# Dividing one 1 MB output store of a batched matmul into three transfers that load the DMA engines unequally

## The chip, the cores and the metric

The kernel runs on one core of one Trainium2 chip. The metric is the device time of one execution in microseconds, the median over several runs. A profile of one execution goes with it. It covers a span a little shorter than the metric, and it names the engines PE (TensorE, matrix multiply), PEld (its weight loads), DVE (VectorE), ACT (ScalarE), POOL (GpSimd) and SP (SyncE, which here only issues transfers and waits). The transfers themselves are carried out by the 16 DMA engines of the core, which all queues share.

## What is computed

```python
def setup_inputs():
    batch, m, k, n = 16, 512, 512, 512
    return {
        "a": np.random.randn(batch, m, k).astype(np.float32),
        "b": np.random.randn(batch, n, k).astype(np.float32),
    }

def reference(a: np.ndarray, b: np.ndarray) -> np.ndarray:
    return np.matmul(a, b.transpose(0, 2, 1)).astype(np.float32)
```

For each of 16 batch elements, a 512 x 512 matrix is multiplied by the transpose of another. Inputs are 32 MiB of float32, outputs 16 MiB, so 48 MiB (50.33 MB) cross between HBM and the core's memory.

## The kernel before, in words

The batch is worked through in eight pairs of two elements. Five programs run beside each other and are tied together by semaphores.

**Loads (SP, L89-L105).** `load(n)` brings in one 2 MB block: for even n the a matrices of pair n/2, for odd n its b matrices. Block n goes to slot n mod 7 of the ring `ld` (NL = 7). The first two blocks are loaded in two halves. From block 7 on a load waits until DVE has begun to cast the block that had the slot (`s_cd`). SP issues the first seven loads at once (L117), and then, in the loop at L119, waits for block n, tells DVE (`s_go`), and issues load n + 6.

**Compute.** DVE casts a block to bf16 into `ha`, `wa`, `hb`, `wb` (L167-L175). PE transposes 128 x 128 tiles against an identity into `tp` (L247). ACT copies the transposed a to `ta` (L206), and DVE the transposed b to `tb` (L187). PE multiplies into `ps` (L266). ACT copies each 128 x 512 result to `ob` (L224), the output ring of NO = 7 slots of one batch element each. Partition p of a slot holds rows 4p to 4p + 3 of the output, 8 KB that lie in one piece in HBM too. ACT raises `s_out` twice per pair: after the first copy of the second element (so the first is complete), and after the last.

**Stores (L110-L115).** `store(n)` waits until `s_out` is n + 1, then writes slot n mod 7 to batch n of the output: one transfer of 128 partitions x 8 KB, which adds 16 to the semaphore `s_st[n]` when it has landed. `landed(n)` (L107) gives the semaphore and the number to wait for. POOL issues stores 0 to 7, in the order that the string `STORES` (L33) writes out: an S is a store, an O a wait for a landed store, which gives ACT a free slot of `ob` (`s_of`). SP issues stores 8 to 15. The table `LATE` (L35) puts stores 8 and 9 behind the wait for load 11, stores 10 and 11 behind load 13, and stores 12 and 13 behind load 15, the last load. Stores 14 and 15 follow (L131, L132).

**End.** SP waits for stores 9 to 14 (L133, L134). A second, otherwise empty section waits for store 15 (L279, L280), and the program ends. Slot 5 of `ob`, which store 12 reads, is not written again afterwards, since batch 19 doesn't exist.

The order around the change is therefore SP's own program order: load 15 has landed, store 12, store 13, store 14, store 15, then the waits. A transfer that SP has issued lies in a queue on each DMA engine that it uses, behind those that SP issued earlier.

Of the kernel before, what the change touches and what calls it, by code (L numbers as in the profile page):

```python
# [10 lines left out]
def kernel(  # L11
# [7 lines left out]
    P = 128  # L19
    batch, M, K = a.shape  # L20
    _, N, _ = b.shape
    J = M // P
# [7 lines left out]
    NO = 7  # L30


    STORES = "SSSSOSOSOSSOOOOOO"  # L33

    LATE = {11: (8, 9), 13: (10, 11), 15: (12, 13)}  # L35

    def sbuf(name, shape, dtype):
        return ctx.enter_context(nc.sbuf_tensor(name, shape, dtype))

    def sem(name):  # L40
        return tc.alloc_semaphore(name)

    with tc.tile_critical(no_gpsimd_drain=True):  # L43
# [8 lines left out]
        ob = sbuf("ob", [P, NO, J, N], f32)  # L52
# [6 lines left out]
        s_st = [sem(f"s_st{i}") for i in range(batch)]  # L59
# [21 lines left out]
            out=ident[:], in_=ident[:], compare_op=mybir.AluOpType.not_equal, fill=1.0,  # L81
# [23 lines left out]
                nc.sync.dma_start(ld[:, slot], src).then_inc(s_ld[slot], 16)  # L105

        def landed(n):  # L107
            return s_st[n], 16

        def store(n):  # L110
            engine = nc.gpsimd if n < STORES.count("S") else nc.sync
            engine.wait_ge(s_out, n + 1)
            engine.dma_start(  # L113
                out[n].rearrange("(p j) n -> p j n", j=J), ob[:, n % NO]
            ).then_inc(s_st[n], 16)  # L115
# [3 lines left out]
        for n in range(2 * pairs):  # L119
            got = nc.sync.wait_ge(s_ld[n % NL], 16 * (n // NL + 1))  # L120
            if n < 2:
                got.then_inc(s_go, 1)
                nc.sync.wait_ge(s_second[n], 16).then_inc(s_go, 1)
            else:
                got.then_inc(s_go, 2)

            if n > 0 and n + NL - 1 < 2 * pairs:
                load(n + NL - 1)
            for m in LATE.get(n, ()):
                store(m)  # L130
        store(batch - 2)  # L131
        store(batch - 1)  # L132
        for n in range(batch - NO, batch - 1):  # L133
            nc.sync.wait_ge(*landed(n))  # L134
# [3 lines left out]
        nc.gpsimd.wait_ge(s_ld[0], 32)  # L138
        for what in STORES:
            if what == "S":  # L140
                store(n_st)
                n_st += 1
            else:
                nc.gpsimd.wait_ge(*landed(n_of)).then_inc(s_of, 1)
                n_of += 1
# [12 lines left out]
        with nc.Fori(0, pairs, engines=[dve]) as u:  # L158
            for x, (h, w, s_c, s_w) in enumerate(
                ((ha, wa, s_ca, s_wa), (hb, wb, s_cb, s_wb))  # L160
            ):
                src = ld[:, bass.ds((u * 2 + x) % NL, 1)].rearrange("p o j k -> p (o j) k")
                take(s_go, 1)
                if x == 0:
# [3 lines left out]
                    out=h[:, :J, :], in_=src[:, :J, :HK]  # L168
# [4 lines left out]
                    out=h[:, J:, :], in_=src[:, J:, :HK]  # L173
                ).then_inc(s_c, 1)
                nc.vector.tensor_copy(  # L175
                    out=w[:, J:, :], in_=src[:, J:, HK:]
                ).then_inc(s_w, 1)
            for ko in range(KO):
# [5 lines left out]
                if ko == 1:  # L184
# [3 lines left out]
                    out=tb[:, ko, :],  # L188
# [9 lines left out]
        with nc.Fori(0, pairs, engines=[act]) as u:  # L198
            for ko in range(KO):
# [5 lines left out]
                for e in range(2):  # L205
                    c = nc.scalar.copy(  # L206
                        out=ta[:, ko, e * J * P:(e + 1) * J * P].rearrange(
                            "k (j p h) -> k j p h", j=J, h=2
                        ),
# [5 lines left out]
            for e in range(2):  # L215
                take(s_of, 1)
                dst = ob[:, bass.ds((u * 2 + e) % NO, 1)].rearrange("m o j n -> m (o j) n")
                for j in range(J):
                    if j < J - 1:
                        nc.scalar.wait_ge(s_mm, j + 1)  # L220
                    else:
# [3 lines left out]
                        out=dst[:, j, :].rearrange("m (p j) -> m p j", j=2 * J),  # L225
# [53 lines left out]
    with tc.tile_critical(no_gpsimd_drain=True):  # L279
        nc.sync.wait_ge(*landed(batch - 1))  # L280
# [30 lines left out]
```

## Time and profile before

| | before |
|---|---|
| time, median of 3 runs | 125.94 us (125.91 to 125.97) |
| the profiled execution | 125.98 us, of which the profile's span is 124.2 us |
| granted TensorE clock, mean | 0.965 |
| PE, PEld busy | 92.5 us (74%), 58.0 us (47%) |
| DVE, ACT busy | 70.0 us (56%), 68.1 us (55%) |
| moved by DMA | 50.33 MB, mean 405 GB/s over the span |
| queue of SP (hardware_dynamic) | 3744 packets, 41.94 MB, 80.2% of 16 engines' span |
| queue of POOL (software_dynamic) | 1152 packets, 8.39 MB, 16.0% |

The rows of busy time tell how long each engine had an instruction in work. The last two rows are the time that packets took on the DMA engines, as a share of all 16 engines' time over the span. A packet here is what one engine moves in one go: 16 KB (one partition of a full load), 8 KB (one partition of a store or of a half load), or 4 bytes (the raising of a semaphore after an engine's part of a transfer).

The profile also records, for each DMA transfer, the 16 moments at which its semaphore was raised, and for each packet its queue, start, duration and size. It does not record which DMA engine moved a packet.

### The profile page before, as it was taken

The numbers are of one execution on the slowest core, as the hardware profiler recorded it, in microseconds if no ns is written. First come the engines' busy times: TensorE is split into PE (matmuls) and PEld (weight loads), VectorE is DVE, ScalarE is ACT, GpSimd is POOL, SyncE is SP. The second block draws the span as 40 slices with busy tenths as digits, with TensorE's granted clock in tenths as the row PEclk, the third lists the DMA queues.
The fourth block names the chain that finished last, engine by engine and source line by source line (L and its number), as shares of the span: only waits on it lengthen the run. The fifth ranks groups of instructions, "written<-read, shape, count | busy, mean of one in ns | idle before, by whom it ended". The sixth has DMA issues, their size and how long they took to land. (4 is left out here: it accounts for less than half of the span.)

```text
span 124.2 us, 2416 instructions
## 1 busy us (share of the span) xinstructions
PE 92.5 (74%) x768; PEld 58.0 (47%) x768; DVE 70.0 (56%) x112; ACT 68.1 (55%) x130; POOL 6.2 (5%) x14
## 2 busy tenths in 40 slices
PE   0006299998999899899989998995699937995000
PEld 0005296467447644764575477343684426541000
DVE  0055676948992897589488578903968059400000
ACT  4005133679558946966695589435665196556000
POOL 2000000000000070002010220000000000000000
PEclk9999999999999999999999999999779999999965
DMA  4999999999999999999999999999999999999970
GB/s 84 401 425 430 443 438 428 433 428 422 428 428 428 428 438 420 401 430 430 414 425 433 430 438 417 435 435 412 454 414 433 409 430 425 430 430 425 428 327 8
DMA packets 4896, 50.33 MB, mean 405 GB/s; under 512 B 544, under 2 KB 544, under 8 KB 544
## 3 DMA queue, kind: packets, MB, share of 16 engines
q1 hardware_dynamic: 3744, 41.94, 80.2%
q0 software_dynamic: 1152, 8.39, 16.0%
HBM read 33.55 MB, written 16.78 MB: 405 GB/s over the span
## 5 line engine op out<-in xcount | busy, mean ns | idle before, releaser
L266 PE MATMUL ps<-tb,ta 128*128 128x512 bf16 x256 | 57.8, 379 | 0.4
L224 ACT COPY ob<-ps 128x512 f32 x64 | 34.4, 589 | 29.7 <-PE ps L266 26.6
L206 ACT COPY ta<-tp 128x512 bf16<-128x512 bf16 x64 | 32.9, 610 | 15.4 <-PE tp L247 15.4
L266 PEld LDWEIGHTS ps<-tb,ta 128*128 128x128 bf16 x256 | 24.2, 98 | 30.5 <-issue 3.9
L247 PE MATMUL tp<-ident,ha 128*128 128x128 bf16 x256 | 20.2, 236 | 12.6 <-PEq L148 12.6
L247 PE MATMUL tp<-ident,hb 128*128 128x128 bf16 x256 | 19.4, 236 | 8.1 <-PEq L148 7.9
L247 PEld LDWEIGHTS tp<-ident,ha 128*128 128x128 bf16 x256 | 17.5, 107 | 15.8 <-issue 14.1
L187 DVE COPY tb<-tp 128x1024 bf16<-128x1024 bf16 x32 | 21.3, 684 | 5.4 <-DVEq L148 5.3
L247 PEld LDWEIGHTS tp<-ident,hb 128*128 128x128 bf16 x256 | 17.2, 107 | 8.7 <-issue 8.7
L167 DVE CAST hb<-ld 128x1024 bf16 x8 | 5.5, 688 | 12.5 <-DVEq L148 12.3
L182 DVE COPY ha<-wa 128x2048 bf16<-128x2048 bf16 x8 | 5.5, 694 | 10.3 <-DVEq L148 10.1
L167 DVE CAST ha<-ld 128x1024 bf16 x8 | 5.5, 687 | 6.6 <-DVEq L148 6.5
L113 POOL DMA_DIRECT2D out_dram<-ob x8 | 5.5, 693 | 65.0 <-DMA ld<-in_b_dram 41.5
L172 DVE CAST hb<-ld 128x1024 bf16 x8 | 5.5, 685 | 1.1 <-DVEq L148 1.1
L172 DVE CAST ha<-ld 128x1024 bf16 x8 | 5.5, 688 | 1.0 <-DVEq L148 1.0
L186 DVE COPY hb<-wb 128x2048 bf16<-128x2048 bf16 x8 | 5.5, 685 | 0.5 <-DVEq L148 0.5
L170 DVE CAST wa<-ld 128x1024 bf16 x8 | 5.5, 686 | 0.0
L170 DVE CAST wb<-ld 128x1024 bf16 x8 | 5.5, 685 | 0.0
L175 DVE CAST wa<-ld 128x1024 bf16 x8 | 5.5, 684 | 0.0
L175 DVE CAST wb<-ld 128x1024 bf16 x8 | 5.5, 682 | 0.0
L197 ACT ACT_TABLE_LOAD x1 | 1.3, 1283 | 1.1 <-SPq L43 1.1
L80 POOL TENSOR_SCALAR_AFFINE_SELECT ident<-ident 128x128 bf16<-128x128 bf16 x1 | 0.3, 283 | 0.2 <-POOL ident L78 0.2
(6 smaller groups left out, 0.8 us busy)
## 6 DMA issues: line engine op xcount, KB each, us to landing
ld<-in_a_dram SPq DMA_DIRECT2D x7, 2048.0 KB, 29.9
ld<-in_b_dram SPq DMA_DIRECT2D x7, 2048.0 KB, 31.1
out_dram<-ob POOLq DMA_DIRECT2D x8, 1024.0 KB, 28.7
out_dram<-ob SPq DMA_DIRECT2D x8, 1024.0 KB, 20.4
ld<-in_a_dram SPq DMA_DIRECT2D x2, 1024.0 KB, 6.2
ld<-in_b_dram SPq DMA_DIRECT2D x2, 1024.0 KB, 10.2
```

The source lines that it names most:

```text
L113: engine.dma_start(out[n].rearrange("(p j) n -> p j n", j=J), ob[:, n % NO]).then_inc(s_st[n], 16)
L167: nc.vector.tensor_copy(out=h[:, :J, :], in_=src[:, :J, :HK]).then_inc(s_cd, 1)
L170: nc.vector.tensor_copy(out=w[:, :J, :], in_=src[:, :J, HK:])
L172: nc.vector.tensor_copy(out=h[:, J:, :], in_=src[:, J:, :HK]).then_inc(s_c, 1)
L175: nc.vector.tensor_copy(out=w[:, J:, :], in_=src[:, J:, HK:]).then_inc(s_w, 1)
L182: nc.vector.tensor_copy(out=ha[:], in_=wa[:]).then_inc(s_ca, 1)
L186: nc.vector.tensor_copy(out=hb[:], in_=wb[:]).then_inc(s_cb, 1)
L187: nc.vector.tensor_copy(out=tb[:, ko, :], in_=tp[:, 2 + ko % 2].rearrange("k j p -> k (j p)"),).then_inc(s_eb, 1)
L206: c = nc.scalar.copy(out=ta[:, ko, e * J * P:(e + 1) * J * P].rearrange("k (j p h) -> k j p h", j=J, h=2), in_=tp[:, ko % 2, :, e * HP:(e ...
L224: c = nc.scalar.copy(out=dst[:, j, :].rearrange("m (p j) -> m p j", j=2 * J), in_=ps[:, j, :].rearrange("m (j p) -> m p j", j=2 * J),)
L247: t = nc.tensor.transpose(tp[:, 2 * x + g, j, :], h[:, j, g * P:(g + 1) * P], ident[:])
L266: t = nc.tensor.matmul(ps[:, j, :], ta[:, ko, (e * J + j) * P:(e * J + j + 1) * P], tb[:, ko, :].rearrange("k (j p) -> k j p", j=2 * J)[:, ...
```

## The change

Store 12 is issued as three transfers in place of one. The first takes the last 2 KB of each of the 128 partitions (row 4p + 3). The second takes the first 6 KB of partitions 0 to 119. The third takes the first 6 KB of partitions 120 to 127. Each of them adds 16 to `s_st[12]`, so the wait for store 12 now asks for 48. The purpose is to give the highest-numbered DMA engine less to carry than the others: 128 partitions divide over 16 engines, 120 over 15, and 8 over 8. All other stores stay as they are, and the same bytes are written.

```diff
     STORES = "SSSSOSOSOSSOOOOOO"
+    FEWER = 12
...
         def landed(n):
-            return s_st[n], 16
+            return s_st[n], 48 if n == FEWER else 16

         def store(n):
             engine = nc.gpsimd if n < STORES.count("S") else nc.sync
             engine.wait_ge(s_out, n + 1)
+            if n == FEWER:
+                dst, src = out[n].rearrange("(p j) n -> p j n", j=J), ob[:, n % NO]
+                for p, j in ((slice(0, P), slice(3, J)), (slice(0, 120), slice(0, 3)), (slice(120, P), slice(0, 3))):
+                    engine.dma_start(dst[p, j], src[p, j]).then_inc(s_st[n], 16)
+                return
             engine.dma_start(
                 out[n].rearrange("(p j) n -> p j n", j=J), ob[:, n % NO]
             ).then_inc(s_st[n], 16)
```

## The prediction

> **What bounds the kernel now.** I read the profile's slices first, to see which resource is full and for how long.
>
> ```profile
> span 124.2 us, 2416 instructions
> DMA  4999999999999999999999999999999999999970
> GB/s 84 401 425 430 443 438 428 433 428 422 428 428 428 428 438 420 401 430 430 414 425 433 430 438 417 435 435 412 454 414 433 409 430 425 430 430 425 428 327 8
> ```
>
> From the second slice to the 38th the DMA engines are 90% busy or more, at about 430 GB/s. Then come one slice of 327 and one of 8. The kernel is bound by its transfers. PE with 74% is not the limit, and the chain that ended last agrees in its own way: it ends with ACT's last copy (113.70 us, 0.58 us long), so the last 9.9 us of the span hold no computing at all. Next I asked for the timeline and for SP's own waits after 112 us:
>
> ```profile
> 114.31 0.33 SPq L113 DMA_DIRECT2D out_dram<-ob  x1
> SPq L134 <- DMA out_dram<-ob: 5.5, 3, 2.4
> SPq L306 <- DMA out_dram<-ob: 1.7, 1, 1.7
> ```
>
> Store 15 is issued at 114.31 us, onto queues that are still full. From then on SP only waits for stores to land, and its last wait (the profile puts it at L306; it is that for store 15) takes 1.7 us. I cut this tail into short windows (window, then the last three columns: clock, DMA share, GB/s):
>
> ```profile
> 119.00:120.00 1.00, 0.00 (x0) 0.00 (x0) 0.00 (x0) 0.00 (x0) 0.00 (x0) 0.50 1.04 442
> 120.30:120.60 0.30, 0.00 (x0) 0.00 (x0) 0.00 (x0) 0.00 (x0) 0.00 (x0) 0.50 0.27 109
> 120.60:121.00 0.40, 0.00 (x0) 0.00 (x0) 0.00 (x0) 0.00 (x0) 0.00 (x0) 0.50 0.06 21
> 121.00:121.50 0.50, 0.00 (x0) 0.00 (x0) 0.00 (x0) 0.00 (x0) 0.00 (x0) 0.50 0.08 33
> 121.50:122.00 0.50, 0.00 (x0) 0.00 (x0) 0.00 (x0) 0.00 (x0) 0.00 (x0) 0.50 0.08 33
> ```
>
> Here is the point of the whole case. A share of 0.06 to 0.08 is one engine of 16. From 120.6 us on, one DMA engine works alone, at its own 27 GB/s. The recorded moments at which store 15's semaphore was raised say the same: 15 of them lie between 120.60 and 120.98 us, the 16th at 122.74 us, 1.76 us after the 15th. The span ends 1.42 us after that (124.165 less 122.74).
>
> How did it fall behind? All engines carry the same bytes. The gap between 15th and 16th raising grows: 0.14 us for the early loads, 0.75 us for store 7 and 1.30 us for store 8 (both near 105 us), 1.60 for store 10, 1.71 for store 12. I split the packet records into 16 gapless sequences (each packet starts 3 ns before its predecessor's end). After 70 us fifteen sequences hold only the standard packets, 309 ns for 8 KB and 611 ns for 16 KB; one holds packets of up to 361 ns, in all 1.37 us too long. So one engine is slow, it is the same one throughout that stretch, and it does not idle. The other fifteen finish their data between 120.26 and 120.65 us, it at 122.27 us.
>
> **What the Trainium skill says.** "DMA: Bandwidth & Descriptors", section "Why a DMA increments its semaphore by 16 and not by 1", says that a transfer from SP runs on the largest number of engines up to 16 that divides its outer dimension, on the lowest-numbered ones, and that each raises the semaphore once, SP adding the rest. By that the three parts run on 16, 15 and 8 engines. The trace before has 16 for every transfer, so no run here shows the other two. The same page, "Latency and other measured facts", calls engines 7 and 15 usually slower than the rest and guesses at the descriptor rings of POOL's transfers. The trace agrees on a slow engine, but shows one, not two, and it is still slow after POOL's last packets (about 104 us). It does not number it. Which of the two it is decides this case.
>
> **The change part by part.** Prices first. Start to start, an 8 KB packet takes 306 ns and a 16 KB packet 608 ns. So 8 KB cost 302 ns and a packet 4 ns: 79.5 ns for 2 KB, 230.5 ns for 6 KB, by this line. Smaller packets are not in the trace. As the other end I take the skill's same page, section "Bandwidth", which gives about 10.5 ns per packet, for loads: 86 and 237 ns. I take 4 ns, since it comes from this trace; 6.5 ns more on 8 or 9 packets is 0.05 to 0.06 us.
>
> *Engine 15* carried 8 packets of 8 KB for store 12, and carries 8 of 2 KB. It loses 48 KB: 6 x 302 = 1.81 us. If it is the slow one, the packets that it loses also carried excess. Its eight packets of store 12 ran 76 ns over; three quarters of that is 0.06 us. Together 1.87 us (1.76 with packets at the dear price and no excess removed).
>
> *Engines 8 to 14* carry 8 of 2 KB and 8 of 6 KB: the same bytes, 8 packets more (32 ns) and one more raising of the semaphore (6 ns start to start). That is 0.04 us, at most 0.09.
>
> *Engines 0 to 7* carry one further packet of 6 KB (0.23 us) and two more raisings: 0.23 + 0.03 + 0.01 = 0.28 us, at most 0.33.
>
> *SP* issues two more transfers. Each issue took 0.332 us, so store 13 goes out 0.66 us later than its 101.64 us. Behind them in SP's program are stores 13, 14 and 15. Store 13 landed only at 116.09 (15th) and 117.80 us, the queues being more than ten microseconds deep, and store 14 waits for ACT until 112.13 us anyway. I cost this at nothing.
>
> *The wait for 48* comes behind the one for store 11 or 12 in SP's list, at about 115 us, and SP has 5 us of slack left. Nothing else waits for store 12: its slot of `ob` is not used again. After store 14, SP has about 0.8 us of barriers (120.28 to 121.07 us) before it waits for store 15. Store 14 would be complete at about 118.8 us, so these move ahead with it and don't bind. Loads have all landed by 100.3 us, so compute moves not at all.
>
> *The sum.* The slow engine's raising goes from 122.74 to 122.74 - 1.87 = 120.87 us. The others lay at 120.60 to 120.98 us; eight of the fifteen get 0.28 us. The latest three lie at 120.95, 120.97 and 120.98 us. With eight of fifteen it's likely that one of the three is among engines 0 to 7, which gives 121.24 us. So the new end is set by engines 0 to 7, not by 15. Last landing 122.74 - 121.24 = 1.50 us earlier, the 1.42 us behind it unchanged: 125.94 - 1.50 = 124.44 us.
>
> A check on the whole: leveling can't beat the mean. The slow engine's 1.75 us divided by 16 is 0.11 us, so perfect balance would end near 120.9 us. The estimate leaves some 0.3 us of that.
>
> **The rivals.**
>
> *A. The slow engine is among 0 to 7 (engine 7).* Then it is given 0.28 us more and nothing is taken away: 125.94 + 0.28 = 126.22 us, up to 126.27. For it: the skill names 7 as much as 15. Against it: when the sequences are followed back to the first load, the slow one begins as the 13th of 16 to start (9th in one of seven ways to resolve ambiguous steps), which suits a late-numbered engine if work is handed out in order. That is an argument, not a proof. 10%.
>
> *B. The slow engine is among 8 to 14, or the lag forms again.* Engine by engine nothing is gained: 125.94 + 0.04 = 125.98 us. The lag forming again is unlikely, since the slow engine's packets after store 12 (24 data packets of stores 13 to 15) run only 0.05 us over in all. 7%.
>
> *C. The relief comes, but small packets cost more than the line says.* A store with 2 KB and 6 KB pieces writes rows with gaps. If each packet cost 50 ns more than by the line, engines 0 to 7 would lose 9 x 0.05 + 0.28 = 0.73 us, ending at 121.7 us, and 124.9 us would result. Against it: the 16 KB and 8 KB packets run at nearly the same rate per byte. 11%.
>
> **How the numbers follow.** The forecast (engine 15 is the slow one, packets by the line) has 72%, and 124.44 us. Within it, the end lies between 121.0 us (no late engine among 0 to 7, that is 1.7 us gained, 124.2 us) and 121.3 us (dear packets, 124.5 us). With differences from run to run I let it reach from 124.1 to 124.7. Adding C, up to 125.1, takes in 83%, and that is the range; A and B stay out. Faster: 72 + 11 = 83%. Slower by over 0.2% (above 126.19 us): A, 10%. Same: B, 7%.
>
> **What would show it.** In the changed kernel the windows after 120.6 us should have no long stretch at a share of 0.06: the DMA share should fall from full to nothing within about 0.8 us. The 16 raisings for store 15 should lie in one group of about 0.7 us, with no straggler, and the last near 121.2 us. Store 12's records should show 128 packets of 2 KB near 80 ns and 128 of 6 KB near 231 ns. Store 11's landing should still show the straggler of 1.7 us, store 13's not. If the straggler remains in store 13 with 1.7 us or more, the wrong engine was relieved. If the packets show 130 and 280 ns, C is right. If the last landing comes early but the span doesn't shrink, my step from landing to end is wrong.

## The result and the profile after

The changed kernel takes 127.54 us (126.82 to 127.86) against 125.95 us: it is slower, by a ratio of 1.0115 (95% interval 1.0072 to 1.0159). The forecast was 124.44 us. A second set of runs gave 127.72 against 125.94 us, 1.0124 (1.0092 to 1.0156).

The slices of the profile after:

```profile
span 125.5 us, 2418 instructions
DMA  4999999999999999999999999999999999999940
GB/s 94 402 425 439 452 418 428 439 428 433 423 433 423 423 415 397 449 418 418 454 402 446 412 449 420 423 446 412 449 405 457 399 431 418 433 403 377 425 209 10
```

The kernel is bound by its transfers as before. But the rate falls to 377 GB/s in the 37th slice (113 to 116 us), where store 12 is carried out, while the profile before has nothing under 401 from the second slice to the 38th, and the tail is longer (209 GB/s in the 39th slice). What the engines moved from 110 to 117 us, in the profile before and then in the one after:

```profile
DMA packets 413, 3.00 MB, mean 428 GB/s; under 512 B 47, under 2 KB 47, under 8 KB 47
DMA packets 534, 2.76 MB, mean 394 GB/s; under 512 B 69, under 2 KB 69, under 8 KB 325
```

SP's issues and its own waits (total, times, longest):

```profile
100.24 1.54 SPq L119 DMA_DIRECT2D out_dram<-ob  x3
SPq L142 <- DMA out_dram<-ob: 6.3, 3, 2.4
SPq L314 <- DMA out_dram<-ob: 1.7, 1, 1.7
```

The three parts are issued in 1.54 us, which delays almost nothing: store 13 goes out at 101.83 us, 0.19 us later than before, and ACT's last copy ends at 114.89 us with 6 us of stores still queued. The last wait reads 1.7 us, as before. That is no sign that nothing changed: it begins some 0.8 us after store 14 has landed, and the same engine is late for stores 14 and 15. The tail in short windows (the last two columns are DMA share and GB/s):

```profile
120.50:121.00 0.50, 0.00 (x0) 0.00 (x0) 0.00 (x0) 0.00 (x0) 0.00 (x0) 0.50 0.36 148
121.00:121.50 0.50, 0.00 (x0) 0.00 (x0) 0.00 (x0) 0.00 (x0) 0.00 (x0) 0.50 0.19 82
121.50:122.00 0.50, 0.00 (x0) 0.00 (x0) 0.00 (x0) 0.00 (x0) 0.00 (x0) 0.50 0.27 115
122.00:122.50 0.50, 0.00 (x0) 0.00 (x0) 0.00 (x0) 0.00 (x0) 0.00 (x0) 0.50 0.12 49
122.50:123.00 0.50, 0.00 (x0) 0.00 (x0) 0.00 (x0) 0.00 (x0) 0.00 (x0) 0.50 0.04 16
123.00:123.50 0.50, 0.00 (x0) 0.00 (x0) 0.00 (x0) 0.00 (x0) 0.00 (x0) 0.50 0.08 33
```

Where one engine alone was late before, now several are (0.19 to 0.27 is three or four of 16), and one of them works alone until 123.7 us. The moments at which store 15's semaphore was raised, in us:

```
before  120.60 ... 120.98 (15 raisings)                                     122.74
after   119.76  120.77 ... 120.96 (8)  121.16 121.25 121.30  122.22 122.57 122.80  124.11
```

Two things stand out. One engine is a microsecond *ahead* of all others: that is the relieved one, and it had not been late. And the straggler is still there, 1.37 us later than before.

I split the packet records into 16 sequences again, now with the three kinds of store 12 (nine packets of 6 KB, eight, or none). The sequence with none (engine 15, by the rule of the Trainium skill that the prediction quotes) shows no excess at all from 70 to 110 us. The one that falls behind there, by 1.13 us, has nine: it is one of engines 0 to 7. Its nine took 239, 234, 245, 426, 339, 460, 481, 775 and 234 ns, 1.33 us over. The first eight belong to the second part of store 12, the last one to the third part. In all, 18 of the 128 packets of 6 KB took 400 ns or more, up to 860 ns. The 2 KB packets took 84 ns.

So there are two theories to test. Theory 1: the wrong engine was relieved, and the slow one got more to carry. Theory 2: engine 15 was the slow one, and the loss has another cause: packets that hinder each other, since 15 and 8 engines read other partitions than 16 do.

### The profile page after: what moved, and what is told of

The parts are those of the page before. It is cut to its first block, busy times and chain, and to the rows that moved or that the text cites. A ratio compares the mean times of both kernels' runs of the same rounds, so it can differ in the third digit from the quotient of the medians.

```text
span 125.5 us, 2418 instructions
## 1 busy us (share of the span) xinstructions
PE 93.7 (75%) x768; PEld 59.3 (47%) x768; DVE 70.2 (56%) x112; ACT 68.1 (54%) x130; POOL 5.9 (5%) x14
## 5 line engine op out<-in xcount | busy, mean ns | idle before, releaser
L255 PE MATMUL tp<-ident,ha 128*128 128x128 bf16 x256 | 20.8, 241 | 12.4 <-PEq L156 12.4
L255 PE MATMUL tp<-ident,hb 128*128 128x128 bf16 x256 | 20.0, 241 | 7.6 <-PEq L156 7.6
L255 PEld LDWEIGHTS tp<-ident,ha 128*128 128x128 bf16 x256 | 18.1, 109 | 15.6 <-issue 14.0
L255 PEld LDWEIGHTS tp<-ident,hb 128*128 128x128 bf16 x256 | 17.8, 110 | 8.2 <-issue 8.2
```

What stands on the lines that cost most here:

```text
L255: t = nc.tensor.transpose(tp[:, 2 * x + g, j, :], h[:, j, g * P:(g + 1) * P], ident[:])
```

## The experiments

The runs were spread over several chips; each group was timed against the kernel before on its own chip (125.82 to 125.95 us throughout). The edits below leave out new buffers and semaphores, and the waits at the end that belong to added or changed transfers.

**Which engine is slow: markers.** `mark_before` adds tiny loads behind store 11, and `mark_after` adds them to the changed kernel.

```diff
+            if n == 13:
+                for i, k in enumerate((2, 4, 6, 7, 8, 11, 14, 15)):
+                    nc.sync.dma_start(mk[:k, i, :32 + 2 * k], a[0, :k, :32 + 2 * k]).then_inc(s_mk, 16)
```

> The kernel before, with eight tiny loads queued by SP behind store 11, on 2, 4, 6, 7, 8, 11, 14 and 15 partitions, each of its own packet size, so that every DMA engine can be told by the markers that it carries. Theory 1 (the slow engine is among 0 to 7, most likely 7): the sequence that falls 1.7 us behind carries the marker of 8 partitions and not that of 7. Theory 2 (it is 15, and the loss has another cause): the slow sequence carries no marker at all. The time should stay within 0.5 us of 125.95 us.

> The same markers in the changed kernel. Theory 1: the slow sequence again carries the marker of 8 and not of 7, and nine 6 KB packets; the sequence without 6 KB packets is free of any lag before store 12 and carries no marker. Theory 2: slow sequence and relieved sequence are one. The markers also tell which engines carried the long 6 KB packets (up to 860 ns in the changed kernel). Time 126.8 to 128.2 us.

They took 126.40 and 126.64 us (one run each), the second a little under the range that I expected. In both, the slow sequence carries the markers of 6, 7, 8 partitions and so on, but not those of 2 and 4: it is engine 4 or 5. The markers do nest (each engine that carries one of few partitions carries those of more), which gives the order of the engines; that the fewest go to the lowest numbers is the rule of the Trainium skill that the prediction quotes, and no run here shows it. The excess of the slow engine's packets from 70 to 110 us is 1.11 us in `mark_before` and 1.19 us in `mark_after`; every other sequence has none in that time. Engine 7 and engine 15 run on time. I had expected engine 7 or 15; both are wrong. In `mark_after` the slow engine meets only one long 6 KB packet (618 ns), and its time lies below every run of the changed kernel itself (126.82 to 128.00 us over both sets).

**Which engine, and does it set the end: more load for the lowest engines.** `extra4`, `extra5` and `extra6` are the kernel before with 40 KB more for each of engines 0 to 3, 0 to 4 and 0 to 5 (written here with k for 4, 5 and 6):

```diff
+            if n == 15:
+                more = a[0].rearrange("(p j) k -> p j k", j=8)
+                for i, (slot, j) in enumerate(((2, 8), (3, 8), (4, 4))):
+                    nc.sync.wait_ge(s_cd, 14)
+                    nc.sync.dma_start(ld[0:4 * k:4, slot, :j], more[:k, :j]).then_inc(s_mk[i], 16)
```

> The kernel before, with 40 KB more to carry for each of engines 0 to 3 (three loads of 4 partitions, 16, 16 and 8 KB each, into free slots of ld, queued by SP behind store 13; each engine writes partitions in steps of 4, so none shares another's). By packet times that is 0.61 + 0.61 + 0.31 = 1.53 us for these engines. By the marker runs the slow engine is 4 or 5, so theory 1 says that the lag of 1.7 us hides it: 125.9 to 126.2 us. If the slow engine is among 0 to 3, or if the end is set by all engines together, 127.2 to 127.5 us.

> The same for engines 0 to 4. Theory 1 with engine 4 slow: 127.3 to 127.5 us. Theory 1 with engine 5 slow: 125.9 to 126.2 us, as with four.

> The same for engines 0 to 5. Theory 1: 127.3 to 127.5 us, since the slow engine, 4 or 5, gets 1.53 us more in either case. If the numbering by markers is wrong and the slow engine is 15, no change: 125.9 to 126.2 us.

| | time, us | ratio (95%) | last raising for store 15 |
|---|---|---|---|
| extra4 | 126.44 | 1.0048 (1.0031 to 1.0065) | 122.84 us |
| extra5 | 127.72 | 1.0151 (1.0134 to 1.0168) | 124.27 us |
| extra6 | 128.01 | 1.0167 (1.0150 to 1.0184) | 124.58 us |

Windows of the tail, first of `extra4`, then of `extra5`:

```profile
121.50:122.00 0.50, 0.00 (x0) 0.00 (x0) 0.00 (x0) 0.00 (x0) 0.00 (x0) 0.50 0.23 98
122.00:122.50 0.50, 0.00 (x0) 0.00 (x0) 0.00 (x0) 0.00 (x0) 0.00 (x0) 0.50 0.04 16
122.50:123.00 0.50, 0.00 (x0) 0.00 (x0) 0.00 (x0) 0.00 (x0) 0.00 (x0) 0.50 0.00 0
```

```profile
122.00:122.50 0.50, 0.00 (x0) 0.00 (x0) 0.00 (x0) 0.00 (x0) 0.00 (x0) 0.50 0.04 16
122.50:123.00 0.50, 0.00 (x0) 0.00 (x0) 0.00 (x0) 0.00 (x0) 0.00 (x0) 0.50 0.08 33
123.00:123.50 0.50, 0.00 (x0) 0.00 (x0) 0.00 (x0) 0.00 (x0) 0.00 (x0) 0.50 0.04 16
123.50:124.00 0.50, 0.00 (x0) 0.00 (x0) 0.00 (x0) 0.00 (x0) 0.00 (x0) 0.50 0.04 16
```

With four engines loaded, they finish at about 122 us, just inside the lag, and the last landing moves by 0.1 us (122.74 to 122.84). The time grew by 0.58 us all the same, more than the 0 to 0.3 us expected; 0.20 us of it is three further waits of SP at the end (from the last landing to the end of the span 1.63 us instead of 1.42), and 0.16 us lies outside the span; about 0.1 us is left unexplained. The fifth engine costs 1.28 us more: the tail now ends with one engine at work until after 123.5 us, and the last landing is 1.53 us later than before (124.27 against 122.74), just what was given to it. The sixth adds 0.29 us where I expected nothing more; why is open. So the slow engine is number 4 in this order, and it sets the end, on this second chip too.

**Does cutting the rows cost: `split16`.** Both parts over 16 engines:

```diff
-                for p, j in ((slice(0, P), slice(3, J)), (slice(0, 120), slice(0, 3)), (slice(120, P), slice(0, 3))):
+                for p, j in ((slice(0, P), slice(3, J)), (slice(0, P), slice(0, 3))):
```

> Store 12 in two transfers, both over 128 partitions and 16 engines: the last 2 KB and the first 6 KB of each partition. Engines stay equally loaded. If cutting the rows is what costs, 127 us or more. If the cost comes from the use of 15 and 8 engines (theory 1 or 2), about 126.0 us (125.9 to 126.1), with all 6 KB packets near 234 ns.

125.91 us, ratio 1.0002 (0.9993 to 1.0011): nothing. No 6 KB packet took over 339 ns, and the slow engine's took 234 to 245 ns. Pieces of 2 KB and 6 KB cost what the line of the prediction said. The loss needs the division over 15 and 8 engines.

**Do the packets hinder each other: `probe`.** After store 15 has landed, parts of batch 12 are written again, one by one, with nothing else moving.

```diff
+        for i, (p, j) in enumerate((
+            (slice(0, P), slice(0, 4)), (slice(0, P), slice(0, 3)), (slice(0, P), slice(3, 4)),
+            (slice(0, 120), slice(0, 3)), (slice(120, P), slice(0, 3)), (slice(0, 32, 4), slice(0, 3)),
+            (slice(120, 124), slice(0, 3)), (slice(0, 28, 4), slice(0, 4)), (slice(0, 112), slice(0, 4)),
+        )):
+            nc.sync.dma_start(dst[p, j], src[p, j]).then_inc(s_pr[i], 16)
+            nc.sync.wait_ge(s_pr[i], 16)
```

> The kernel before, and after the last store has landed parts of batch 12 are written again from the same slot, one after another, each waited for. Nothing else moves then. If 6 KB packets are long because of which partitions an engine reads, they are long here too: 6 KB from 8 neighbouring partitions over 8 engines above 450 ns a packet, from 4 neighbouring ones over 4 engines also, from 8 partitions in steps of 4 about 234 ns; 6 KB of 128 partitions over 16 engines 234 ns, of 120 over 15 some longer than 234 ns. If they are long only because of the queues around them, every 6 KB packet takes about 234 ns here. The time grows by the probes, by 20 to 35 us.

Two windows of it, the first over the 6 KB packets of 128 partitions on 16 engines, the second over those of 120 on 15 (last columns DMA share, GB/s):

```profile
127.40:129.60 2.20, 0.00 (x0) 0.00 (x0) 0.00 (x0) 0.00 (x0) 0.00 (x0) 0.50 0.88 357
133.10:136.60 3.50, 0.00 (x0) 0.00 (x0) 0.00 (x0) 0.00 (x0) 0.00 (x0) 0.50 0.79 211
```

Engines are nearly as busy in the second window and move little more than half as much per time. By the packet records:

| transfer, alone | 6 KB packets: mean (longest), ns |
|---|---|
| 128 partitions, 16 engines | 241 (256) |
| 120 partitions, 15 engines | 369 (675) |
| partitions 120 to 127, 8 engines | 771 (895) |
| partitions 120 to 123, 4 engines | 659 (735) |
| partitions 0, 4, ... 28, 8 engines | 236 (236) |

The second half of theory 2 holds: packets hinder each other. Eight engines on neighbouring partitions took more than three times as long for a packet as eight on partitions in steps of 4. The probe changes the rows written in HBM along with the partitions read; `eight_ports`, below, changes the partitions alone. I take it that 128 partitions are spread over the engines so that this doesn't arise and 120 are not, but the records don't show which engine reads which partition. 112 partitions of 8 KB over 16 engines were held up too (mean 396 ns, up to 844, against 317 ns for 128).

**Which part of store 12 hinders: `eight_ports`, `no_eight`, `fewer15`, beside the changed kernel again.** The first reads the third part from partitions in steps of 4 (part of batch 12 then holds other rows' values), the second leaves the third part out (part of batch 12 is not written), and the third divides store 15 in place of store 12.

```diff
# eight_ports
-                    engine.dma_start(dst[p, j], src[p, j]).then_inc(s_st[n], 16)
+                    engine.dma_start(dst[p, j], src[slice(0, 32, 4) if p.start else p, j]).then_inc(s_st[n], 16)
# no_eight
-                for p, j in ((slice(0, P), slice(3, J)), (slice(0, 120), slice(0, 3)), (slice(120, P), slice(0, 3))):
+                for p, j in ((slice(0, P), slice(3, J)), (slice(0, 120), slice(0, 3))):
# fewer15
-    FEWER = 12
+    FEWER = 15
```

> The changed kernel, but the third part of store 12 reads partitions 0, 4, ... 28 in place of 120 to 127, and writes them where those would go (so 24 rows of batch 12 are another's; bytes, engines and destinations are the same). Theory: neighbouring partitions hinder each other, and the third part's packets are 550 to 900 ns for that reason: then they fall to about 235 ns here, and the time by 0.2 to 0.6 us, to about 126.9 to 127.3 us on a chip where the changed kernel takes 127.5 us. What stays above 126.2 us is the second part's. If the wrong engine's extra load alone makes the loss, no difference to the changed kernel.

> The changed kernel once more, so that the others of this group can be set against it on the same chip: 127.0 to 127.9 us.

> The changed kernel without the third part of store 12 (the first 6 KB of partitions 120 to 127 are not written). The slow engine then carries as many bytes as in the kernel before. If its extra 6 KB were the loss, the time is back at 125.9 to 126.1 us. If the second part's 6 KB packets are held up because 15 engines read partitions that others read too, the most of the loss stays: 126.6 to 127.4 us.

> The same division, of store 15 in place of store 12. Store 15 is the last, so when the slow engine, 1.7 us behind, comes to its late 6 KB packets, the other engines have nothing more to read. If its packets are held up by the reads of the next store on the other engines, they fall to about 234 ns here, and the loss to the extra 6 KB: 126.1 to 126.5 us. If 6 KB packets over 15 engines are dear by themselves, as dear as in the changed kernel: 127.2 to 127.8 us.

| | time, us | ratio (95%) | mean span less that of the kernel before |
|---|---|---|---|
| after_again | 127.72 (126.96 to 128.00) | 1.0124 (1.0092 to 1.0156) | 125.65 - 124.14 = 1.51 us |
| eight_ports | 127.22 (126.21 to 127.25) | 1.0091 (1.0063 to 1.0119) | 125.07 - 124.06 = 1.01 us |
| no_eight | 126.79 (126.15 to 127.25) | 1.0077 (1.0056 to 1.0098) | 124.92 - 124.14 = 0.78 us |
| fewer15 | 126.45 (126.38 to 126.84) | 1.0045 (1.0028 to 1.0063) | 124.58 - 124.14 = 0.44 us |

Without its third part, and with the same bytes on the slow engine as before, the changed kernel still loses about half: the 120 partitions over 15 engines alone are worth some 0.78 us. With the third part read in steps of 4 it is 0.23 us more, the size of one 6 KB packet, and with neighbouring partitions another 0.50 us. But single runs of these kernels lie up to 1.1 us apart, `eight_ports` was on another chip, and the intervals of neighbouring rows overlap, so neither the steps nor their order are settled. What the runs support is that the second part alone costs time, and that the same division in store 15 costs less than in store 12.

The packets of `eight_ports` settle one point. Those of the third part can be told by a raising of the semaphore on either side: there each took 234 ns, with the rows in HBM as in the changed kernel, where some took 428 and 860 ns. So it is the partitions read that made them long. In the changed kernel's profile the slow engine's own packet of the third part took 234 ns too; its long ones were all of the second part.

`fewer15` bears on when the hold-up arises. Its last landing comes at 123.08 us, 0.34 us later than before, near the 0.28 us that the extra load alone was to cost. Its late engine comes to its 6 KB packets after the others have finished. Its tail:

```profile
121.00:121.50 0.50, 0.00 (x0) 0.00 (x0) 0.00 (x0) 0.00 (x0) 0.00 (x0) 0.50 0.06 25
121.50:122.00 0.50, 0.00 (x0) 0.00 (x0) 0.00 (x0) 0.00 (x0) 0.00 (x0) 0.50 0.06 25
122.00:122.50 0.50, 0.00 (x0) 0.00 (x0) 0.00 (x0) 0.00 (x0) 0.00 (x0) 0.50 0.06 25
```

One engine, at a steady rate: its last five 6 KB packets took 234 ns each. None of the 128 took more than 348 ns, against 860 in the changed kernel. In the changed kernel the late engine's long ones (426 to 775 ns) start between 113.63 and 115.35 us, and by then most engines are in store 13. Their 8 KB packets are held up too: between 110 and 118 us five take above 370 ns, up to 529, where the kernel before has none above 335. That fits a collision of the late engine's reads for the odd division with the regular reads of the next store, but it is an argument: no run moves the next store away and leaves the rest. What stays open is why the other fourteen hardly hinder each other in `fewer15`, when they do so in the quiet of `probe`, where all start at one time.

**Helping the engine that is slow: `relief4`.** Store 15 is divided by columns; the last part of the work goes to engines 0 to 3.

```diff
+                dst = out[n].rearrange("(p j) n -> p (j n)", j=J)
+                src = ob[:, n % NO].rearrange("p j n -> p (j n)")
+                for p, j in ((slice(0, P), slice(256, 2048)), (slice(0, 124), slice(0, 256)), (slice(124, P), slice(0, 256))):
```

> A try at helping the engine that is slow, number 4. Store 15: 7 KB of each partition over all 16 engines, then the first 1 KB of 124 partitions over engines 0 to 3 (124 divides by 4), and that of the last 4 over 4. Engines 4 to 15 carry 8 KB less (0.30 us), engines 0 to 3 carry 32 KB more instead and 32 packets more (about 1.2 us less 0.3, plus 0.1), which fits inside the lag of 1.7 us. If engine 4 sets the end, 125.5 to 125.7 us against 125.86 to 125.95 us before. If packets of engines 0 to 3 are held up by shared partitions, 125.9 to 126.6 us.

125.85 against 125.94 us, ratio 0.9998 (0.9989 to 1.0006): no change that can be told, where I expected 125.5 to 125.7 us. The windows of its tail:

```profile
121.00:121.50 0.50, 0.00 (x0) 0.00 (x0) 0.00 (x0) 0.00 (x0) 0.00 (x0) 0.50 0.33 119
121.50:122.00 0.50, 0.00 (x0) 0.00 (x0) 0.00 (x0) 0.00 (x0) 0.00 (x0) 0.50 0.06 23
122.00:122.50 0.50, 0.00 (x0) 0.00 (x0) 0.00 (x0) 0.00 (x0) 0.00 (x0) 0.50 0.00 0
```

Inside the span it did what it should: the four helpers (share 0.33) end at 121.4 to 121.7 us, the slow engine at 121.94 us, and the last landing comes at 122.41 us, 0.33 us earlier than before. The mean span is 0.19 us shorter (123.95 against 124.14). But the time outside the span went from 1.80 to 1.95 us and took most of it back. The changed kernel, `eight_ports` and `fewer15` show the same 1.95 us, `no_eight` and `split16` the 1.80 to 1.82 us of the kernel before. What makes that difference I don't know; it isn't the number of transfers, since `mark_before` has eight more and 1.80 us, and `mark_after`, with the three parts besides, 1.84 us (one run each).

**Why engine 4 is slow: `all_sp`.** POOL issues no transfer; its eight stores go out on SP's queue.

```diff
-    STORES = "SSSSOSOSOSSOOOOOO"
+    STORES = "OOOOOOOOO"
-    LATE = {11: (8, 9), 13: (10, 11), 15: (12, 13)}
+    LATE = {7: (0, 1, 2, 3), 9: (4,), 10: (5,), 11: (6, 7, 8, 9), 13: (10, 11), 15: (12, 13)}
```

> The kernel before with stores 0 to 7 issued by SP too (0 to 3 behind the wait for load 7, 4 behind load 9, 5 behind load 10, 6 and 7 behind load 11), so that POOL issues no transfer at all and one queue carries everything. The early stores now stand behind loads in one queue and land later, so the time as such may be longer (126 to 132 us). What is looked at is the lag: if engine 4 is slow because of POOL's queue, all 16 raisings of each late store lie within 0.6 us. If it is slow for another reason, the 16th still comes 1 to 2 us after the 15th.

131.98 us, ratio 1.0476 (1.0442 to 1.0509), as the early stores stand behind loads. The lag forms without POOL's queue: the 16th raising comes 0.16 us after the 15th for store 4, then 0.29, 0.42, 0.66, 0.88, 1.01, 1.13 and 1.32 us for stores 5 to 11, and 1.09 and 1.23 us for stores 12 and 13. So POOL's transfers are not what it takes. (Which engine it was is not marked here.) Four windows of `all_sp` (busy time of PE comes second, DMA share and GB/s last):

```profile
100.00:110.00 10.00, 9.45 (x90) 5.98 (x89) 7.12 (x12) 7.51 (x15) 0.00 (x0) 1.00 1.01 425
114.00:122.00 8.00, 7.45 (x66) 4.33 (x64) 3.67 (x6) 5.74 (x12) 0.00 (x0) 1.00 0.41 167
122.00:126.00 4.00, 2.30 (x11) 0.86 (x9) 0.00 (x0) 2.17 (x4) 0.00 (x0) 1.00 0.59 240
126.00:129.00 3.00, 0.00 (x0) 0.00 (x0) 0.00 (x0) 0.00 (x0) 0.00 (x0) 0.84 0.91 380
```

The lag grows in the first, with PE busy. In the pause of the second the queues run dry, and in the last, with no engine computing, stores 14 and 15 land with 0.03 and 0.02 us between the 15th and the 16th. In the kernel before, too, engine 4's packets run little over once PE has ended (0.05 us in stores 13 to 15). A link to the computing is possible; no run separates it from other causes, and why it is engine 4 stays open.

## Why the prediction was wrong

**The view of the bound was right.** The last landing of store 15 sets the end, and one DMA engine sets that landing. `extra4` and `extra5` show it: the same 1.53 us of load moves the last landing by 0.1 us on engines that are not late, and by the whole 1.53 us once engine 4 carries it too.

**The step that failed: "If it is the slow one" for engine 15.** I gave that 72%, on the strength of a general statement of the Trainium skill ("DMA: Bandwidth & Descriptors", "Latency and other measured facts"), which calls 7 and 15 usually slower, and of the order in which sequences first started (13th of 16). Neither carries a number of an engine from this kernel. The engine is number 4; 7 and 15 ran on time. So 1.81 us of packets were taken off an engine that was not late, and the slow one got more to carry. The other statement that I took from that page ("Why a DMA increments its semaphore by 16 and not by 1") fits as far as the runs can tell: a transfer over k engines uses the lowest-numbered ones. The markers nest as they then must, and the engines raised the semaphore of store 12's three parts 16, 15 and 8 times.

**A term that was mis-sized: rival A was right in kind and too small.** It said that a slow engine among 0 to 7 would cost 0.28 us (126.22 us). It named number 7, with the same load as 4. Measured were 1.59 us. The term that was too small is the price of a 6 KB packet over 15 and 8 engines. I took 230.5 ns from a line through 8 KB and 16 KB packets, with 237 ns as the other end; both come from transfers that are spread over 16 engines. `split16` shows that this is right for 16 engines. Over 15 and 8, the slow engine's nine packets took 1.33 us more, in the profiled run. Together with the 0.28 us, and 0.13 us less excess on its other packets, that makes 1.48 us; its data ended at 123.72 instead of 122.27 us, 1.45 us later.

**Rival C and rival A were not alternatives.** C allowed 50 ns more for each packet. The mean over the 128 packets of 6 KB is just that, 6.66 us / 128 = 52 ns. But it falls unevenly, and the late engine had 147 ns a packet. I gave A and C separate chances and added C only to the forecast, so my range had no place for both at once.

**Costed at nothing, and rightly as far as the profile shows:** SP's two further issues, the wait for 48, the loads and the compute. One reading in it was wrong without harm: the two issues took 0.64 and 0.48 us and not 0.33 us each, yet they moved store 13 by 0.19 us and not by 0.66, as SP had waited for ACT from 100.66 to 101.64 us before. A part of 0.15 us of the loss lies outside the span; no step of mine had it.

**What would have shown it** was listed, and in part did. The straggler stayed in store 13, the sign of the wrong engine: it came at 119.18 us, where it had come at 117.80 before. But it was 1.27 us behind the 15th, not 1.7, because others were late as well. Of the sign of C one half came: the 6 KB packets took 286 ns on average, while those of 2 KB stayed at 84 ns.

## What to carry to other kernels

That one DMA engine lags can be read from the 16 raisings of a semaphore; which one it is cannot, so mark it first, with tiny transfers over different numbers of partitions, before building a division of work on it. A transfer over 120 or 8 neighbouring partitions is not 15/16 or 1/16 of one over 128: alone on the core, its packets took one and a half to over three times as long on average here, and in the kernel some packets of the next store were long as well (up to 529 ns). So compare packet durations before dividing. And where two rivals add up, the range has to hold their sum.

## What the runs showed of the hardware that I had not expected

- Engine 4 of 16, in the order that the markers give, is slow in this kernel: its packets run 1.1 us over from 70 to 110 us, where no other's do. Markers on one chip leave 4 or 5, the extra loads on another say 4, and `relief4` on a third fits it. On a fourth chip, without POOL's transfers, a lag of 1.3 us formed too.
- With nothing else moving, 6 KB packets from eight neighbouring partitions over eight engines took 771 ns on average, and 236 ns from eight partitions in steps of 4.
- The time outside the profiled span was 1.95 us for some kernels and 1.80 us for others, which decided whether a span 0.19 us shorter could be seen in the metric.
